# Rotary embedding on one core: hand-placed semaphores, eight of sixteen positions a batch summed on TensorE, and one signed GpSimd product per tile

## The chip, the cores and the metric

The kernel runs on one core of a Trainium2 chip. The time is in device microseconds of one execution, here the median of several runs. A core has TensorE (PE in the profile, its weight loads are PEld), VectorE (DVE), ScalarE (ACT), GpSimd (POOL) and SyncE (SP). SP and ACT also issue the DMAs here; their queues appear as SPq and ACTq, and 16 DMA engines move the data.

## The reference

```python
def reference(x, cos, sin):        # x: 8 x 2048 x 8 x 64, cos and sin: 2048 x 32, all f32
    x1 = x[..., : x.shape[-1] // 2]
    x2 = x[..., x.shape[-1] // 2 :]
    cos = cos[None, :, None, :]
    sin = sin[None, :, None, :]
    out1 = x1 * cos - x2 * sin
    out2 = x1 * sin + x2 * cos
    return np.concatenate([out1, out2], axis=-1)
```

Each of the 8 batches has 2048 positions of 8 heads of 64 numbers. The first 32 numbers of a head are x1, the last 32 x2. So the output is x times cosine, plus x with its halves exchanged times sine, with the sign of the first half turned. The input is 33.55 MB and so is the output.

## The kernel before

Position index q x 16 + r lies on partition q, so that each of the 128 partitions holds 16 positions of a batch, 512 numbers (2 KB) each: 32 KB in a row, in SBUF and in memory. A batch is one tile `xt` of 128x8192, of which there are five (`NBUF`), and it is rotated in place. The loads of batches 0 to 4 are issued by SP at the start (line 67; batch 0 in three parts); the load of batch b + 5 is issued after batch b's work and waits until batch b's store has left the buffer. Stores (line 74) are issued by ACT, those of the last batch by SP. The first batch is stored in shares of 2, 6 and 8 positions (4, 12 and 16 KB a partition), the last in shares of 8, 4 and 4, the others whole.

A batch is worked in pieces, of four positions mostly (`UNIT`, 2048 columns). Each piece is of one of three kinds, and `kinds` names the five that aren't A:

- A: GpSimd makes the sine products in two instructions, one per half of the heads (line 124), into an SBUF tile `t2`; VectorE makes the cosine product into the PSUM tile `t1` (line 131) and adds both into `xt` (line 138).
- B (batches 2, 4, 5, first piece): the cosine product goes to SBUF instead, and TensorE adds: two matmuls with the identity `eye` accumulate t1 and t2 in a PSUM tile `o` of 1024 columns (lines 145, 146), and ScalarE copies it back into `xt` (line 147).
- C (batches 1, 3, first piece): VectorE makes the sine product too (line 150), without exchange or sign; TensorE reads the crossed halves, with `eye` or the negative `neye` (lines 162, 163), and ScalarE copies (line 167).

There is one buffer of `o`, so a sum waits for the copy before it. A matmul of 512 columns of f32 shows as two records in the profile. The order of instructions on each engine is the order of the program (`keep`); the semaphores between engines are placed by the framework. Small tables are made at the start: `nsin`, `neye`, and copies of cosine and sine in PSUM (lines 92 to 95).

Of the kernel before, what the change touches and what calls it, by code (L numbers as in the profile page):

```python
# [9 lines left out]
@with_exitstack  # L10
def kernel(
    ctx: ExitStack,
    tc: tile.TileContext,
    x: bass.AP,
    cos: bass.AP,
    sin: bass.AP,
    out: bass.AP,
):
    nc = tc.nc
    keep = tc.keep_in_program_order  # L20
    f32 = mybir.dt.float32
    PSUM = bass.MemoryType.PSUM

    B, S, H, D = x.shape
    Dh = D // 2
    P = 128
    HD = H * D
    R = S // P
    ROW = R * HD
    UNIT = 4 * HD  # L30
    NBUF = 5
    C = 512
    last = B - 1

    xv = x.rearrange("b (q r) h d -> b q (r h d)", q=P)
    ov = out.rearrange("b (q r) h d -> b q (r h d)", q=P)
    cos_src = cos.rearrange("(q r) d -> q r d", q=P)
    sin_src = sin.rearrange("(q r) d -> q r d", q=P)

    const_pool = ctx.enter_context(tc.tile_pool(name="const", bufs=1))  # L40
    tab_pool = ctx.enter_context(tc.tile_pool(name="tab", bufs=1, space=PSUM))
    t1_pool = ctx.enter_context(tc.tile_pool(name="t1p", bufs=1, space=PSUM))
    o_pool = ctx.enter_context(tc.tile_pool(name="op", bufs=1, space=PSUM))
    t1s_pool = ctx.enter_context(tc.tile_pool(name="t1s", bufs=2))
    xpool = ctx.enter_context(tc.tile_pool(name="xpool", bufs=NBUF))
    t2_pool = ctx.enter_context(tc.tile_pool(name="t2p", bufs=3))

    cos_sb = const_pool.tile([P, R, Dh], f32, tag="cb")
    sin_sb = const_pool.tile([P, R, Dh], f32, tag="sb")
    nsin = const_pool.tile([P, R, Dh], f32, tag="ns")  # L50
    eye = const_pool.tile([P, P], f32, tag="eye")
    neye = const_pool.tile([P, P], f32, tag="neye")
    cos_ps = tab_pool.tile([P, R, Dh], f32, tag="cp")
    sin_ps = tab_pool.tile([P, R, Dh], f32, tag="sp")

    xts = {}

    def spans(sizes):
        lo = 0
        for n in sizes:  # L60
            yield lo, n
            lo += n

    def load(b):
        xt = xpool.tile([P, ROW], f32, tag="xt", name=f"xt{b}")
        for lo, n in spans([UNIT, UNIT, 2 * UNIT] if b == 0 else [ROW]):
            keep(nc.sync.dma_start(out=xt[:, lo : lo + n], in_=xv[b, :, lo : lo + n]))  # L67
            if b == 0 and lo == 0:
                keep(nc.sync.dma_start(out=cos_sb, in_=cos_src))
        xts[b] = xt  # L70

    def store(b, lo, n):
        queue = nc.sync if b == last else nc.scalar
        keep(queue.dma_start(out=ov[b, :, lo : lo + n], in_=xts[b][:, lo : lo + n]))  # L74

    keep(nc.scalar.dma_start(out=sin_sb, in_=sin_src))
    for b in range(NBUF):
        load(b)

    keep(nc.vector.addr_align(128))  # L80
    keep(nc.gpsimd.addr_align(128, offset=120))
    keep(nc.gpsimd.memset(eye, 0.0))  # L82
    nc.gpsimd.affine_select(
        out=eye,
        in_=eye,
        compare_op=mybir.AluOpType.not_equal,
        fill=1.0,
        base=0,
        pattern=[[-1, P]],
        channel_multiplier=1,  # L90
    )
    keep(nc.scalar.mul(nsin, sin_sb, -1.0))  # L92
    keep(nc.scalar.copy(sin_ps, sin_sb))  # L93
    keep(nc.scalar.mul(neye, eye, -1.0))
    keep(nc.vector.tensor_copy(cos_ps, cos_sb))  # L95

    def rep(a, n):
        return dataclasses.replace(a, ap=[a.ap[0][:], a.ap[1][:], [0, n], a.ap[-1][:]])

    kinds = {}  # L100
    for b, kind in ((1, "C"), (2, "B"), (3, "C"), (4, "B"), (5, "B")):
        kinds[(b, 0)] = kind

    def rotate(b, lo, n):
        kind = kinds.get((b, lo), "A")
        xt = xts[b][:, lo : lo + n]
        r0 = lo // HD
        nr = n // HD
        xk = xt.rearrange("p (r k d) -> p r k d", r=nr, d=Dh)
        xu = xt.rearrange("p (g u d) -> p g u d", u=2, d=Dh)  # L110
        if kind == "A":
            t1 = t1_pool.tile([P, n], f32, tag="t1")
        else:
            t1 = t1s_pool.tile([P, n], f32, tag="t1s")
        if kind == "C":
            t2 = t1s_pool.tile([P, n], f32, tag="t1s")
        else:
            t2 = t2_pool.tile([P, n], f32, tag="t2")
        t1u = t1.rearrange("p (g u d) -> p g u d", u=2, d=Dh)
        t2u = t2.rearrange("p (g u d) -> p g u d", u=2, d=Dh)  # L120
        if kind != "C":
            for u, tab in ((1, sin_sb), (0, nsin)):
                keep(
                    nc.gpsimd.tensor_mul(  # L124
                        out=t2u[:, :, u, :].rearrange("p (r h) d -> p r h d", h=H),
                        in0=xu[:, :, 1 - u, :].rearrange("p (r h) d -> p r h d", h=H),
                        in1=rep(tab[:, r0 : r0 + nr, :], H),
                    )
                )
        keep(  # L130
            nc.vector.tensor_mul(  # L131
                out=t1.rearrange("p (r k d) -> p r k d", r=nr, d=Dh),
                in0=xk,
                in1=rep(cos_ps[:, r0 : r0 + nr, :], 2 * H),
            )
        )
        if kind == "A":
            keep(nc.vector.tensor_add(out=xt, in0=t1, in1=t2))  # L138
        elif kind == "B":
            for j in range(n // (2 * C)):  # L140
                o = o_pool.tile([P, 2 * C], f32, tag="o")
                for k in range(2):
                    cs = slice((2 * j + k) * C, (2 * j + k + 1) * C)
                    oc = o[:, k * C : (k + 1) * C]
                    nc.tensor.matmul(oc, eye, t1[:, cs], start=True, stop=False)  # L145
                    nc.tensor.matmul(oc, eye, t2[:, cs], start=False, stop=True)  # L146
                keep(nc.scalar.copy(xt[:, 2 * j * C : 2 * (j + 1) * C], o))  # L147
        else:
            keep(
                nc.vector.tensor_mul(  # L150
                    out=t2.rearrange("p (r k d) -> p r k d", r=nr, d=Dh),
                    in0=xk,
                    in1=rep(sin_ps[:, r0 : r0 + nr, :], 2 * H),
                )
            )
            G = C // Dh
            for u in range(2):
                o = o_pool.tile([P, n // 2], f32, tag="o")
                for j in range(n // 2 // C):
                    oc = o[:, j * C : (j + 1) * C]  # L160
                    gs = slice(j * G, (j + 1) * G)
                    nc.tensor.matmul(oc, eye, t1u[:, gs, u, :], start=True, stop=False)  # L162
                    nc.tensor.matmul(  # L163
                        oc, eye if u else neye, t2u[:, gs, 1 - u, :], start=False, stop=True
                    )
                keep(
                    nc.scalar.copy(  # L167
                        xu[:, :, u, :], o.rearrange("p (g d) -> p g d", d=Dh)
                    )
                )  # L170

    def pieces(b):
        if b == 0:
            return [2 * HD, 2 * HD, UNIT, UNIT, UNIT]
        if b == last:
            return [UNIT, UNIT, UNIT, 2 * HD, 2 * HD]
        return [UNIT] * 4

    def shares(b):
        if b == 0:  # L180
            return [2 * HD, UNIT + 2 * HD, 2 * UNIT]
        if b == last:
            return [2 * UNIT, UNIT, UNIT]
        return [ROW]

    for b in range(B):
        done = 0
        outs = list(spans(shares(b)))
        for lo, n in spans(pieces(b)):
            rotate(b, lo, n)  # L190
            done = lo + n
            while outs and sum(outs[0]) <= done:
                store(b, *outs.pop(0))
        if b + NBUF <= last:
            load(b + NBUF)


# [28 lines left out]
```

## Time and profile before

| | |
|---|---|
| median of 3 runs | 163.44 us (163.33 to 163.69) |
| profiled execution, its own time | 163.48 us |
| its span | 161.7 us |
| VectorE busy | 140.1 us (87%) |
| GpSimd busy | 138.8 us (86%) |
| TensorE busy | 49.6 us (31%) |
| ScalarE busy | 12.8 us (8%) |
| bytes moved by the DMA engines | 67.65 MB, 418 GB/s over the span |

All times in the views are microseconds from the start of the span. The page has the busy share of each engine in 40 equal slices (a digit is tenths; the granted TensorE clock and the DMA's share are given in the same way), the chain of waits that ended last, and groups of instructions: line, engine, operation, output from inputs, shapes, count, busy time, mean duration in ns, then the idle time before them and what ended it. The timeline lists start, duration and instruction. A DMA issue shows on its queue with its line.

### The profile page before, as it was taken

The page shows a single profiled execution, that of the slowest core. Times are in us where ns is not written, and L with a number is a line of the kernel's source. Part 1 is how long each engine was busy: PE and PEld are TensorE (multiplying, and loading weights), DVE is VectorE, ACT ScalarE, POOL GpSimd, SP SyncE. Part 2 cuts the span into 40 slices and gives each one's busy share as a digit, 9 for nine tenths or more (in the row PEclk, how much of TensorE's full clock was granted, in tenths as well). Part 3 has the DMA queues.
Part 4 walks back from the last instruction along what each step waited for, and adds up shares of the span by engine and source line. Part 5 has one row for each costly group of instructions (what it writes and reads, how often), then busy time and mean ns, then how long its engine had stood idle before and what let it go on. Part 6 is the DMA issues. An engine that isn't in the chain of part 4 may idle for free.

```text
span 161.7 us, 573 instructions
## 1 busy us (share of the span) xinstructions
PE 49.6 (31%) x80; PEld 18.7 (12%) x80; DVE 140.1 (87%) x66; ACT 12.8 (8%) x14; POOL 138.8 (86%) x70
## 2 busy tenths in 40 slices
PE   0000000597309760978049723973000000000000
PEld 0000000142004220322023302320000000000000
DVE  0297999999999999999999999199989999899950
ACT  3300000002200220021100220022000000000000
POOL 1399994999999999992999979999799997999800
PEclk9999999999975998589956995599655555555555
DMA  5999999999999999999999999999999999999995
GB/s 184 418 432 438 420 428 405 444 409 489 397 401 450 438 462 397 438 462 397 438 462 397 438 462 397 438 470 389 438 470 389 438 470 397 430 470 397 405 420 213
DMA packets 3458, 67.65 MB, mean 418 GB/s; under 512 B 384, under 2 KB 384, under 8 KB 768
## 3 DMA queue, kind: packets, MB, share of 16 engines
q1 hardware_dynamic: 2016, 38.01, 55.4%
q10 hardware_dynamic: 1440, 29.62, 42.7%
q14 instruction: 2, 0.02, 0.0%
HBM read 34.08 MB, written 33.55 MB: 418 GB/s over the span
## 4 chain that ended last, share of the span: by engine, by line
DMA 48%; DVE 37%; POOL 9%; issue 2%; DVEq 0%; SPq 0%; POOLq 0%; ACTq 0%
DMA xt<-in_x_dram 26%; DMA out_dram<-xt 19%; DVE t L131 18%; DVE xt L138 17%; POOL t L124 9%; DMA sin_sb<-in_sin_dram 4%; DVE t L150 1%; DVEq L138 0%; SPq L67 0%; POOLq L124 0%; ACTq L74 0%
## 5 line engine op out<-in xcount | busy, mean ns | idle before, releaser
L124 POOL TENSOR_TENSOR t<-xt,sin_sb 128x1024 f32<-128x1024 f32 (+1 forms) x32 | 70.5, 2203 | 11.3 <-DMA xt<-in_x_dram 5.2
L131 DVE TENSOR_TENSOR t<-xt,cos_ps 128x2048 f32<-128x2048 f32 (+1 forms) x34 | 73.4, 2167 | 0.8
L124 POOL TENSOR_TENSOR t<-xt,nsin 128x1024 f32<-128x1024 f32 (+1 forms) x32 | 70.5, 2202 | 0.0
L138 DVE TENSOR_TENSOR xt<-t,t 128x2048 f32<-128x2048 f32 (+1 forms) x29 | 62.2, 2145 | 8.0 <-POOL t L124 5.4
L145 PE MATMUL o<-t,eye 128*128 128x512 f32 x24 | 17.2, 807 | 22.9 <-DVE t L131 19.5
L162 PE MATMUL o<-t,eye 128*128 128x512 f32 x16 | 12.1, 847 | 37.7 <-DVE t L131 35.5
L146 PE MATMUL o<-t,eye 128*128 128x512 f32 x24 | 14.9, 709 | 0.0
L147 ACT COPY xt<-o 128x1024 f32<-128x1024 f32 x6 | 6.1, 1012 | 45.7 <-PE o L146 45.7
L145 PEld LDWEIGHTS o<-t,eye 128*128 128x128 f32 x24 | 5.6, 257 | 32.3 <-issue 26.4
L162 PEld LDWEIGHTS o<-t,eye 128*128 128x128 f32 x16 | 3.7, 256 | 43.1 <-issue 39.3
L167 ACT COPY xt<-o 128x1024 f32<-128x1024 f32 x4 | 4.0, 1012 | 47.8 <-PE o L163 36.8
L95 DVE COPY cos_ps<-cos_sb 128x512 f32<-128x512 f32 x1 | 0.7, 695 | 6.9 <-DMA cos_sb<-in_cos_dram 6.9
L146 PEld LDWEIGHTS o<-t,eye 128*128 128x128 f32 x24 | 5.7, 239 | 8.2 <-issue 7.7
L163 PE MATMUL o<-t,neye 128*128 128x512 f32 x8 | 6.3, 882 | 0.2 <-DVE t L150 0.2
L150 DVE TENSOR_TENSOR t<-xt,sin_ps 128x2048 f32<-128x2048 f32 x2 | 4.6, 2281 | 0.0
L163 PE MATMUL o<-t,eye 128*128 128x512 f32 x8 | 4.1, 592 | 0.0
L163 PEld LDWEIGHTS o<-t,neye 128*128 128x128 f32 x8 | 2.2, 306 | 5.3 <-issue 3.7
L82 POOL MEMSET eye<- 128x128 f32 x1 | 0.2, 204 | 2.4 <-issue 2.4
L163 PEld LDWEIGHTS o<-t,eye 128*128 128x128 f32 x8 | 1.5, 190 | 1.9 <-issue 1.9
L92 ACT ACT_TABLE_LOAD x1 | 1.3, 1283 | 1.2 <-PEq L210 1.2
L92 ACT ACTIVATE nsin<-sin_sb 128x512 f32<-128x512 f32 x1 | 0.6, 629 | 4.0 <-DMA sin_sb<-in_sin_dram 4.0
L93 ACT COPY sin_ps<-sin_sb 128x512 f32<-128x512 f32 x1 | 0.6, 579 | 0.0
(6 smaller groups left out, 1.0 us busy)
## 6 DMA issues: line engine op xcount, KB each, us to landing
xt<-in_x_dram SPq DMA_DIRECT2D x7, 4096.0 KB, 41.4
out_dram<-xt ACTq DMA_DIRECT2D x6, 4096.0 KB, 28.6
xt<-in_x_dram SPq DMA_DIRECT2D x2, 1024.0 KB, 6.9
xt<-in_x_dram SPq DMA_DIRECT2D x1, 2048.0 KB, 13.1
out_dram<-xt ACTq DMA_DIRECT2D x1, 2048.0 KB, 25.8
out_dram<-xt SPq DMA_DIRECT2D x1, 2048.0 KB, 10.0
out_dram<-xt SPq DMA_DIRECT2D x2, 1024.0 KB, 6.3
out_dram<-xt ACTq DMA_DIRECT2D x1, 1536.0 KB, 20.7
```

The lines of the kernel that those rows point to most:

```text
L92: keep(nc.scalar.mul(nsin, sin_sb, -1.0))
L95: keep(nc.vector.tensor_copy(cos_ps, cos_sb))
L124: nc.gpsimd.tensor_mul(out=t2u[:, :, u, :].rearrange("p (r h) d -> p r h d", h=H), in0=xu[:, :, 1 - u, :].rearrange("p (r h) d -> p r h d" ...
L131: nc.vector.tensor_mul(out=t1.rearrange("p (r k d) -> p r k d", r=nr, d=Dh), in0=xk, in1=rep(cos_ps[:, r0 : r0 + nr, :], 2 * H),)
L138: keep(nc.vector.tensor_add(out=xt, in0=t1, in1=t2))
L145: nc.tensor.matmul(oc, eye, t1[:, cs], start=True, stop=False)
L146: nc.tensor.matmul(oc, eye, t2[:, cs], start=False, stop=True)
L147: keep(nc.scalar.copy(xt[:, 2 * j * C : 2 * (j + 1) * C], o))
L150: nc.vector.tensor_mul(out=t2.rearrange("p (r k d) -> p r k d", r=nr, d=Dh), in0=xk, in1=rep(sin_ps[:, r0 : r0 + nr, :], 2 * H),)
L162: nc.tensor.matmul(oc, eye, t1u[:, gs, u, :], start=True, stop=False)
L163: nc.tensor.matmul(oc, eye if u else neye, t2u[:, gs, 1 - u, :], start=False, stop=True)
L167: nc.scalar.copy(xu[:, :, u, :], o.rearrange("p (g d) -> p g d", d=Dh))
```

## The change

The framework's placement of semaphores is replaced by semaphores placed by hand, inside one critical section: `Count` holds a semaphore and what it has been raised to, and `wait` makes an engine wait for such a point. Buffers are fixed: one `t2` of four quarters of 2048 columns, one `t1` and one `o` in PSUM; a plan for each batch gives kind, first position, number of positions, and quarter.

- Eight positions of batches 0 to 6 and four of batch 7 are summed on TensorE: in odd batches one C piece of eight positions, in even ones two B pieces of four. The cosine product of a B or C piece is written over `xt`; TensorE reads `xt` and `t2`.
- GpSimd makes the sine products of a piece in one instruction, from a table `sgn` that holds the negative and the positive sine side by side, and with a backward step over the halves of `xt`. The first piece of batch 0 is still made in two.
- Batch 0 is stored in four shares of four positions (8 KB a partition), in the order 0, 4, 12, 8.
- ScalarE copies the cosine table instead of VectorE; two alignment calls are dropped; SP waits for the last stores at the end.

Core of the diff (`Count` counts, `repeat`, `region` and `products` give views of a table, of `xt` and of `t2`):

```diff
-    t1_pool = ctx.enter_context(tc.tile_pool(name="t1p", bufs=1, space=PSUM))
-    o_pool = ctx.enter_context(tc.tile_pool(name="op", bufs=1, space=PSUM))
-    t1s_pool = ctx.enter_context(tc.tile_pool(name="t1s", bufs=2))
...
+    t2 = sb("t2", [4 * UNIT])
+    t1 = psum.tile([P, UNIT], f32, tag="t1", name="t1")
+    cos_ps = psum.tile([P, R, Dh], f32, tag="cp", name="cos_ps")
+    sin_ps = psum.tile([P, R, Dh], f32, tag="sp", name="sin_ps")
+    o = psum.tile([P, 2 * C], f32, tag="o", name="o")
...
+    def wait(engine, point):
+        engine.wait_ge(point[0].sem, point[1])
+    crit = tc.tile_critical(no_gpsimd_drain=True)
+    crit.__enter__()
+    dve, prod, mm, act = (Count(n) for n in ("dve", "prod", "mm", "act"))
+    pair = [Count(f"pair{i}") for i in range(4)]
+    landed = {}
+    stored = {}
+    read = [None] * 4
+    known = {"gpsimd": set(), "vector": set()}
...
     def load(b):
+        parts = [(0, 4), (4, 4), (8, 8)] if b == 0 else [(0, R)]
+        if b >= NBUF:
+            for point in stored[b - NBUF]:
+                wait(nc.sync, point)
+        for lo, n in parts:
+            cols = slice(lo * HD, (lo + n) * HD)
+            ins = nc.sync.dma_start(out=xts[b % NBUF][:, cols], in_=xv[b, :, cols])
+            point = Count(f"ld{b}_{lo}").by(ins, 16)
+            for r in range(lo, lo + n):
+                landed[(b, r)] = point
             if b == 0 and lo == 0:
-                keep(nc.sync.dma_start(out=cos_sb, in_=cos_src))
-        xts[b] = xt
-    def store(b, lo, n):
-        queue = nc.sync if b == last else nc.scalar
-        keep(queue.dma_start(out=ov[b, :, lo : lo + n], in_=xts[b][:, lo : lo + n]))
-    keep(nc.scalar.dma_start(out=sin_sb, in_=sin_src))
-    for b in range(NBUF):
+                cos_in = Count("cos_in").by(nc.sync.dma_start(out=cos_sb, in_=cos_src), 16)
+        return cos_in if b == 0 else None
+    def store(b, lo, n, needs):
+        engine = nc.sync if b == last else nc.scalar
+        for point in needs:
+            wait(engine, point)
+        cols = slice(lo * HD, (lo + n) * HD)
+        ins = engine.dma_start(out=ov[b, :, cols], in_=xts[b % NBUF][:, cols])
+        stored.setdefault(b, []).append(Count(f"st{b}_{lo}").by(ins, 16))
...
-    keep(nc.vector.addr_align(128))
-    keep(nc.gpsimd.addr_align(128, offset=120))
...
-    keep(nc.scalar.mul(nsin, sin_sb, -1.0))
-    keep(nc.scalar.copy(sin_ps, sin_sb))
-    keep(nc.scalar.mul(neye, eye, -1.0))
-    keep(nc.vector.tensor_copy(cos_ps, cos_sb))
+    wait(nc.scalar, sin_in)
+    nsin_done = act.by(nc.scalar.mul(sgn[:, :, 0, :], sin_sb, -1.0))
+    wait(nc.scalar, cos_in)
+    cos_done = act.by(nc.scalar.copy(cos_ps, cos_sb))
+    sgn_done = act.by(nc.scalar.copy(sgn[:, :, 1, :], sin_sb))
+    sin_done = act.by(nc.scalar.copy(sin_ps, sin_sb))
+    wait(nc.scalar, eye_done)
...
+    def sines(b, lo, n, buf, count):
+        xt = region(b, lo, n)
+        if read[buf]:
+            wait(nc.gpsimd, read[buf])
+        if landed[(b, lo)] not in known["gpsimd"]:
+            known["gpsimd"].add(landed[(b, lo)])
+            wait(nc.gpsimd, landed[(b, lo)])
+        if (b, lo) == (0, 0):
+            xu = xt.rearrange("p (g u d) -> p g u d", u=2, d=Dh)
+            tu = products(buf, n).rearrange("p (g u d) -> p g u d", u=2, d=Dh)
+            for u, tab in ((1, sin_sb), (0, sgn[:, :, 0, :])):
+                wait(nc.gpsimd, sin_in if u else nsin_done)
+                done = count.by(
                     nc.gpsimd.tensor_mul(
+                        out=tu[:, :, u, :].rearrange("p (r h) d -> p r h d", h=H),
                         in0=xu[:, :, 1 - u, :].rearrange("p (r h) d -> p r h d", h=H),
+                        in1=repeat(tab[:, lo : lo + n, :], H),
                     )
                 )
+            wait(nc.gpsimd, sgn_done)
+            return done
+        x5 = xt.rearrange("p (r h u d) -> p r h u d", r=n, h=H, u=2)
+        swapped = dataclasses.replace(
+            x5, offset=x5.offset + Dh, ap=[d[:] for d in x5.ap[:3]] + [[-Dh, 2], x5.ap[4][:]]
+        )
+        return count.by(
+            nc.gpsimd.tensor_mul(
+                out=products(buf, n).rearrange("p (r h u d) -> p r h u d", r=n, h=H, u=2),
+                in0=swapped,
+                in1=repeat(sgn[:, lo : lo + n], H),
             )
         )
...
+    def times(out, table, b, lo, n):
+        return nc.vector.tensor_mul(
+            out=out.rearrange("p (r k d) -> p r k d", r=n, d=Dh),
+            in0=region(b, lo, n).rearrange("p (r k d) -> p r k d", r=n, d=Dh),
+            in1=repeat(table[:, lo : lo + n, :], 2 * H),
+        )
+    t1_read = cos_done
+    self_known = 0
+    copied = neye_done
+    def vector_waits(*points):
+        nonlocal self_known
+        for point in points:
+            if point in known["vector"] or (point[0] is dve and point[1] <= self_known):
+                continue
+            if point[0] is dve:
+                self_known = point[1]
+            wait(nc.vector, point)
+    def on_vector(b, lo, n, buf):
+        nonlocal t1_read
+        sines(b, lo, n, buf, pair[buf])
+        vector_waits(landed[(b, lo)], t1_read)
+        known["vector"].add(landed[(b, lo)])
+        wait(nc.vector, pair[buf].by(times(t1[:, : n * HD], cos_ps, b, lo, n)))
+        t1_read = read[buf] = dve.by(
+            nc.vector.tensor_add(out=region(b, lo, n), in0=t1[:, : n * HD], in1=products(buf, n))
+        )
+        return t1_read
+    def on_tensor(b, lo, n, buf, crossed=False):
+        nonlocal copied
+        if crossed:
+            vector_waits(landed[(b, lo)], *read[buf : buf + n // 4], sin_done)
+            made = dve.by(times(products(buf, n), sin_ps, b, lo, n))
+            vector_waits(made)
         else:
+            made = sines(b, lo, n, buf, prod)
+            wait(nc.vector, made)
+        known["vector"].add(landed[(b, lo)])
+        wait(nc.tensor, dve.by(times(region(b, lo, n), cos_ps, b, lo, n)))
+        for j in range(0, n, 2):
+            wait(nc.tensor, copied)
+            cs = slice(j * HD, (j + 2) * HD)
+            xj, tj = region(b, lo, n)[:, cs], products(buf, n)[:, cs]
+            pattern = "p (u g d) -> p u g d" if crossed else "p (g u d) -> p g u d"
+            if crossed:
+                xu = xj.rearrange("p (g u d) -> p u g d", u=2, d=Dh)
+                tu = tj.rearrange("p (g u d) -> p u g d", u=2, d=Dh)
+            for k in range(2):
+                oc = o[:, k * C : (k + 1) * C]
+                xk = xu[:, k] if crossed else xj[:, k * C : (k + 1) * C]
+                tk = tu[:, 1 - k] if crossed else tj[:, k * C : (k + 1) * C]
+                nc.tensor.matmul(oc, eye, xk, start=True, stop=False)
+                sign = neye if crossed and k == 0 else eye
+                ins = nc.tensor.matmul(oc, sign, tk, start=False, stop=True)
+            summed = mm.by(ins)
+            wait(nc.scalar, summed)
+            out = xu if crossed else xj
+            src = o.rearrange("p (u g d) -> p u g d", u=2, d=Dh) if crossed else o
+            copied = act.by(nc.scalar.copy(out, src))
+            read[buf + j // 4] = summed
+        return copied
+    wait(nc.tensor, eye_done)
+    for b in range(B):
         if b == 0:
+            plan = [("A", 0, 4, 0), ("B", 4, 4, 2), ("B", 8, 4, 3), ("A", 12, 4, 1)]
+            shares = [(0, 4), (4, 4), (12, 4), (8, 4)]
+        elif b == last:
+            plan = [("B", 0, 4, 2), ("A", 4, 4, 0), ("A", 8, 4, 1), ("A", 12, 4, 0)]
+            shares = [(0, 8), (8, 4), (12, 4)]
+        elif b % 2:
+            plan = [("C", 0, 8, 0), ("A", 8, 4, 2), ("A", 12, 4, 3)]
+            shares = [(0, R)]
+        else:
+            plan = [("B", 0, 4, 2), ("A", 4, 4, 0), ("B", 8, 4, 3), ("A", 12, 4, 1)]
+            shares = [(0, R)]
+        done = {}
+        for kind, lo, n, buf in plan:
+            point = on_vector(b, lo, n, buf) if kind == "A" else on_tensor(b, lo, n, buf, kind == "C")
+            for r in range(lo, lo + n):
+                done[r] = point
+            while shares and all(r in done for r in range(shares[0][0], sum(shares[0]))):
+                s0, sn = shares.pop(0)
+                needs = {}
+                for r in range(s0, s0 + sn):
+                    count, v = done[r]
+                    needs[count] = max(v, needs.get(count, 0))
+                store(b, s0, sn, needs.items())
         if b + NBUF <= last:
             load(b + NBUF)
+    for b in range(last + 1 - NBUF, B):
+        for point in stored[b]:
+            wait(nc.sync, point)
+    crit.__exit__(None, None, None)
```

## The prediction

> **What bounds the kernel now.** I read the slices and the chain of waits first, then TensorE's and ScalarE's timeline, then the stretches at the end.
>
> ```profile
> DMA  5999999999999999999999999999999999999995
> ...
> DMA packets 3458, 67.65 MB, mean 418 GB/s; under 512 B 384, under 2 KB 384, under 8 KB 768
> ...
> DMA 48%; DVE 37%; POOL 9%; issue 2%; DVEq 0%; SPq 0%; POOLq 0%; ACTq 0%
> ```
>
> The 16 DMA engines are full in all 40 slices but the first and the last. 67.65 MB at 418 GB/s is the span, 161.7 us. The chain that ended last runs through loads, stores and vector work in turn, so compute (DVE 140.1 us busy, POOL 138.8) only just keeps up. No edit can make the bytes fewer; an edit gains little and loses whatever stops the DMA.
>
> ```profile
> 155.00:156.00 1.00, 0.00 (x0) 0.00 (x0) 0.83 (x1) 0.00 (x0) 0.00 (x0) 0.50 0.99 418
> ...
> 159.00:160.00 1.00, 0.00 (x0) 0.00 (x0) 0.00 (x0) 0.00 (x0) 0.00 (x0) 0.50 0.65 270
> 160.00:161.00 1.00, 0.00 (x0) 0.00 (x0) 0.00 (x0) 0.00 (x0) 0.00 (x0) 0.50 0.02 8
> ```
>
> In this view by stretches the last two columns are the DMA share and GB/s. The data end at 159.65 (0.65 of that microsecond), so a tail of 161.70 - 159.65 = 2.05 us follows the last byte. From 140 to 156, stores nearly alone, the rate is 422 to 425 GB/s; I use 425. In the first 4 us the core moved 174 GB/s x 4 = 0.70 MB, worth 1.6 us at full rate, so 2.4 us were lost; the first issue was at 0.74, so a queue that starts empty costs 2.4 - 0.74, about 1.6 us.
>
> What the change loads most is TensorE with ScalarE. Their timeline in one of the five pieces summed there today:
>
> ```profile
> 48.52 2.05 PE L145 MATMUL o<-t,eye 128*128 128x512 f32 x2 [6.73 <-DVE t L131]
> 50.36 1.91 PE L146 MATMUL o<-t,eye 128*128 128x512 f32 x2
> 52.07 1.58 PE L145 MATMUL o<-t,eye 128*128 128x512 f32 x2
> 53.48 1.02 PE L146 MATMUL o<-t,eye 128*128 128x512 f32 x2
> 55.65 1.12 PE L145 MATMUL o<-t,eye 128*128 128x512 f32 x2 [1.15 <-ACT xt L147]
> 56.62 1.02 PE L146 MATMUL o<-t,eye 128*128 128x512 f32 x2
> 57.47 1.02 PE L145 MATMUL o<-t,eye 128*128 128x512 f32 x2
> 58.33 1.02 PE L146 MATMUL o<-t,eye 128*128 128x512 f32 x2
> ```
>
> ```profile
> 54.59 1.01 ACT L147 COPY xt<-o 128x1024 f32<-128x1024 f32 x1 [11.74 <-PE o L146]
> 59.39 1.01 ACT L147 COPY xt<-o 128x1024 f32<-128x1024 f32 x1 [3.79 <-PE o L146]
> ```
>
> Columns: start, duration, what, and the idle time before it. A tile is 1024 columns (two positions). There is one o buffer, so TensorE waits out the copy (1.15 us idle) and ScalarE waits out the sum (3.79): the two take turns. A warm tile has a period of 59.39 - 54.59 = **4.80 us**. The crossed pieces have the same period (copies at 37.03 and 41.83, 71.41 and 76.22). The first tile of a piece is slow: 6.07 us from first matmul to copy, not 3.74.
>
> **The change, part by part.**
>
> *More positions on TensorE.* Today five pieces of four positions, ten tiles. After: batch 0 sums 8 positions, batches 1 to 6 sum 8 each, batch 7 sums 4: 60 positions, **30 tiles**, still one o, still an explicit wait of TensorE for the copy. 30 x 4.80 = 144 us in one serial chain, 19.2 us a batch. That is nearly the time that the DMA needs for a batch (8.39 MB at 425 GB/s, 19.7 us); the chain cannot win time back, and it starts late and has a tail.
>
> *Where it starts.* POOL's first (split) product runs 6.49 to 8.77 to 11.05 (two 128x1024 forms, 2.28 us apart on the timeline). The first TensorE piece, positions 4 to 7, needs the signed product, then the vector product, which now writes x in place and so must wait for POOL.
>
> ```profile
> L131 DVE TENSOR_TENSOR t<-xt,cos_ps 128x2048 f32<-128x2048 f32 x30 | 68.5, 2292 | 0.7
> L124 POOL TENSOR_TENSOR t<-xt,sin_sb 128x1024 f32<-128x1024 f32 x28 | 65.5, 2339 | 8.2 <-DMA xt<-in_x_dram 5.2 <-DVE xt L138 3.0
> L124 POOL TENSOR_TENSOR t<-xt,sin_sb 128x512 f32<-128x512 f32 x4 | 5.0, 1256 | 3.1 <-DMA sin_sb<-in_sin_dram 3.1
> ```
>
> The signed product, 128x2048 in one instruction, is not in the trace. The two POOL rows give 2339 - 1256 = 1083 ns per 512 elements; three more steps on 1256 give 4.50 us, two halves give 4.56. Bounds: as fast as VectorE, 2.29, or twice its price for the backward step, 9.1. I take 4.56, since inner runs (32 elements) and elements are those of today. So 11.05 + 4.56 = 15.6, + 2.35 (2.29 and a semaphore) = 18.0. First copy at 18.0 + 6.07 = 24.0, done at 25.0.
>
> *Is it kept fed?* Each piece's data against the moment when TensorE is free for it: batch 0 second piece 22.5 against 29.8; batch 1: its load lands near 27.3 as now, two vector products of 4.48 (4096 elements at the slope of the rows) give 36.3 against 39.4; batch 2 51.9 and 61.0 against 58.6 and 68.2. From there it repeats: the last plain piece of batch 2 waits for t2 buffer 1, which TensorE frees at 57.5, is added at 65.7, and then VectorE makes batch 3's 8 positions by 74.7 against 77.8; batch 5 111.9 against 116.2; batch 7 150.9 against 154.6. The leads are 3 to 9 us: narrow, never negative. So the chain has no gap: last copy ends at 25.0 + 29 x 4.80 = **164.2**.
>
> *The last stores.* Batch 6's store needs the 28th copy, 154.6. Batch 7's first store, positions 0 to 7, contains its summed piece and heads SP's queue, so the other two stores stand behind it though their adds end near 160 and 165: all 4.19 MB go after 164.3. The DMA idles before 154.7 (batch 5's store, issued at 135.4, is done by 135.5 + 1.6 + 9.9 = 147). Then 154.7 + 1.6 + 8.39 MB / 425 GB/s (19.7) = 176.0, + 2.05 = span **178.1**. The span now is 161.70 inside an execution of 163.48, so 1.78 lies around it: **179.9 us**, against that execution's 163.48 and the median's 163.44.
>
> The Trainium skill, "DMA: Bandwidth & Descriptors", section "Where 436 GB/s comes from", says that HBM to SBUF transfers bind near 358 GB/s. By it the last 8.39 MB would take 23.4 us and the sum would be 183.6. This trace, with 418 GB/s over the whole span, disagrees.
>
> *What costs nothing, and why.* VectorE falls from 61 large products and sums to 55 (some 126 us for 140), POOL from 32 to 26 (117 for 139): both now wait on TensorE's buffers, so nothing is gained. Positions 0 to 3 are stored together, at about 13.5 and not 10.25, and batch 0's last piece goes at 39.4 instead of 27.8, since ScalarE, which issues stores, has the four copies ahead of it. Load 5 waits for these: about 61 instead of 53.66. The cover is loads 1 to 4, in the queue until 21.5 + 4.2 MB are moved (61); load 5 lands near 80, and its first product starts after 100. Without that cover the DMA would idle some 2 us. Cos copied by ScalarE: ready at 7.65, VectorE now starts at 7.64. The dropped alignment calls have no row; the "issue" gaps in the chain are 0.02 to 0.07 us, I take 0.
>
> *Hand-placed waits.* Semaphore hops in a tile are 0.04 and 0.05 us now. If they vanished, 30 x 0.09 = 2.7 us are won; if each becomes 0.06 longer, 3.6 are lost. I take 0 and keep both ends.
>
> **Rivals.**
>
> *The clock falls back in the chain.* If every piece starts with a slow tile, as all five now do, 14 x (6.07 - 3.70) = 33 us are added: copies end at 197.4, then 1.7 + 9.9 + 2.05 + 1.78: 212.8. For: the granted clock is 0.50 from 48.5 to 53 and 0.99 from 53 to 60.4. Against: the slow tiles follow pauses of over 5 us; after the 1.1 us pauses every second tile was fast, and the new chain has only those.
> The Trainium skill, "TensorE: Matmul & The Clock Gate", section "A second HAM failure mode: psum-queue depth-cycling", says that short pauses between groups on PSUM buffers can make the clock swing; by it this rival, or part of it, comes. Ten tiles of this trace do not show it.
>
> *The signed product is dearer.* At 6.0 us POOL gates the pieces: last copies at 159.5 (batch 6) and 169.1, giving 184.8. At 9.1, POOL sets the pace, the last add ends at 240.9, and 248.9 follows.
>
> *The chain does not bind (no slower).* Place: the o buffer between TensorE and ScalarE. If the period were at most 4.24 us, copies would end by 148.1 and the 4.19 MB behind them (1.7 + 9.9 + 2.05) at 161.7; then the full DMA decides again: about 163.4, or some tenths less for the faster last batch. It needs the copy to run beside the next sum. For: 3.70 and 1.01 apart would fit. Against: the wait is written out, and the pause is in the trace. The matmul count would show whether 30 tiles were indeed summed.
>
> **Numbers.** Gap-free chain 0.76, 179.9 (own range 176 to 185: waits, rate between 418 and 442, a microsecond at the start). Product near 6 us 0.07 (184.8), at 9.1 0.03 (248.9); clock 0.09 (212.8); chain hidden 0.05 (163.4). The range 175 to 188 holds the first two, nearly all of 0.83. A difference under 0.2% can't be told from none in this kernel; faster by more has 0.03 and within it 0.02, both from the last case, slower 0.95.
>
> **What would show it.** Right: 30 copies on ScalarE, 4.80 us apart, idle before them put down to TensorE; DMA share falling below 0.9 from about 130; SP's last three stores issued together at 164. Wrong at the start: the first copy far from 24. Wrong in the middle: gaps in the copies (VectorE or POOL late), or a POOL product off 4.5 us. Wrong altogether: DMA full to the end with copies under 4.3 us apart.

## The result and the profile after

The changed kernel takes 181.40 us (median of 4 runs, 180.73 to 181.92); the kernel before, run beside it, takes 163.51. The ratio is 1.109, with a 95% interval of 1.105 to 1.114. The profiled execution took 181.72, its span is 179.3.

The first view is the page of the changed kernel, busy tenths in 40 slices of 4.5 us, then the totals of the DMA.

```profile
PE   0000977777777888777777777778887777774000
...
PEclk9999999999999999999999999999999999999755
DMA  5999999999999989999999999999908850499991
...
DMA packets 3602, 67.67 MB, mean 377 GB/s; under 512 B 400, under 2 KB 400, under 8 KB 656
```

The bytes are the same (67.67 MB), but the DMA row has holes: from slice 30 on the engines are idle, then full, then idle. TensorE is busy at an even 0.7 to 0.8 from slice 6 to slice 36, and the granted clock reads full all that time.

Four groups of the same page, the costliest first:

```profile
L169 POOL TENSOR_TENSOR t<-xt,sgn 128x2048 f32<-128x2048 f32 x25 | 112.8, 4532 | 38.0 <-PE o L235 38.0
L233 PE MATMUL o<-xt,eye 128*128 128x512 f32 x120 | 65.0, 624 | 51.2 <-ACT xt L240 30.6
L240 ACT COPY xt<-o 128x1024 f32<-128x1024 f32 x30 | 30.4, 1012 | 124.8 <-PE o L235 124.8
L177 DVE TENSOR_TENSOR xt<-xt,cos_ps 128x2048 f32<-128x2048 f32 (+1 forms) x12 | 33.9, 2821 | 24.5 <-POOL t L169 24.4
```

There are the 30 copies. ScalarE idled 124.8 us ahead of them, all of it waiting for TensorE's sums, and TensorE idled 30.6 us waiting for the copies: each waits for the other. The signed product takes 4.53 us, and GpSimd now idles 38.0 us for quarters of `t2` that TensorE has still to read: the engine that was 86% busy waits for the one that was 31% busy.

ScalarE's timeline, its first four copies and the last four:

```profile
23.41 1.01 ACT L240 COPY xt<-o 128x1024 f32<-128x1024 f32 x1 [14.22 <-PE o L235]
28.22 1.01 ACT L240 COPY xt<-o 128x1024 f32<-128x1024 f32 x1 [3.79 <-PE o L235]
...
33.08 1.01 ACT L240 COPY xt<-o 128x1024 f32<-128x1024 f32 x1 [3.85 <-PE o L235]
37.88 1.01 ACT L240 COPY xt<-o 128x1024 f32<-128x1024 f32 x1 [3.79 <-PE o L235]
...
148.91 1.01 ACT L240 COPY xt<-o 128x1024 f32<-128x1024 f32 x1 [3.85 <-PE o L235]
153.71 1.01 ACT L240 COPY xt<-o 128x1024 f32<-128x1024 f32 x1 [3.79 <-PE o L235]
154.75 0.34 ACTq L103 DMA_DIRECT2D out_dram<-xt  x1
158.58 1.01 ACT L240 COPY xt<-o 128x1024 f32<-128x1024 f32 x1 [3.85 <-PE o L235]
163.38 1.01 ACT L240 COPY xt<-o 128x1024 f32<-128x1024 f32 x1 [3.79 <-PE o L235]
```

The idle time ahead of a copy is 3.79 us, or 3.85 at the start of a piece, from the second copy to the last: a period of 4.80 or 4.86 us, without one gap in 140 us. Batch 6's store leaves at 154.75, right behind the 28th copy.

The last stretches (the columns are those of the view shown of before: engines' busy times, granted clock, DMA share, GB/s):

```profile
130.00:135.00 5.00, 3.70 (x8) 1.44 (x8) 2.81 (x2) 1.21 (x2) 4.41 (x2) 1.00 0.08 33
135.00:145.00 10.00, 7.37 (x16) 2.88 (x16) 5.65 (x3) 2.36 (x3) 4.87 (x2) 1.00 0.98 419
145.00:155.00 10.00, 7.50 (x17) 3.04 (x18) 6.33 (x3) 2.08 (x3) 10.00 (x3) 1.00 0.00 0
155.00:165.00 10.00, 7.24 (x16) 2.71 (x16) 9.63 (x5) 2.02 (x2) 7.08 (x2) 1.00 0.97 415
```

Batch 5's store fills the DMA from 135 to 145, then there is nothing to store until 155. About 15 us of an idle DMA, from 130 on, are most of what the change costs.

### The profile page after: what moved, and what is told of

It is laid out like the page before. It is cut to its first block, busy times and chain, and to the rows that moved or that the text cites. A ratio compares the mean times of both kernels' runs of the same rounds, so it can differ in the third digit from the quotient of the medians.

```text
span 179.3 us, 716 instructions
## 1 busy us (share of the span) xinstructions
PE 112.1 (63%) x240; PEld 43.8 (24%) x240; DVE 124.1 (69%) x49; ACT 34.1 (19%) x36; POOL 118.1 (66%) x33
## 2 busy tenths in 40 slices
DMA packets 3602, 67.67 MB, mean 377 GB/s; under 512 B 400, under 2 KB 400, under 8 KB 656
## 4 chain that ended last, share of the span: by engine, by line
PE 30%; DVE 28%; POOL 22%; ACT 6%; DMA 3%; issue 3%; DVEq 0%; SPq 0%; POOLq 0%
POOL t L169 20%; PE o L233 16%; PE o L235 14%; DVE t L177 11%; DVE xt L204 9%; DVE xt L177 7%; ACT xt L240 6%; DMA xt<-in_x_dram 3%; POOL t L156 2%; DVEq L71 0%; POOLq L71 0%; SPq L301 0%; SPq L74 0%
## 5 line engine op out<-in xcount | busy, mean ns | idle before, releaser
L169 POOL TENSOR_TENSOR t<-xt,sgn 128x2048 f32<-128x2048 f32 x25 | 112.8, 4532 | 38.0 <-PE o L235 38.0
L233 PE MATMUL o<-xt,eye 128*128 128x512 f32 x120 | 65.0, 624 | 51.2 <-ACT xt L240 30.6
L240 ACT COPY xt<-o 128x1024 f32<-128x1024 f32 x30 | 30.4, 1012 | 124.8 <-PE o L235 124.8
L177 DVE TENSOR_TENSOR xt<-xt,cos_ps 128x2048 f32<-128x2048 f32 (+1 forms) x12 | 33.9, 2821 | 24.5 <-POOL t L169 24.4
L177 DVE TENSOR_TENSOR t<-xt,cos_ps 128x2048 f32<-128x2048 f32 x17 | 39.0, 2291 | 8.2 <-ACT cos_ps L126 8.0
L204 DVE TENSOR_TENSOR xt<-t,t 128x2048 f32<-128x2048 f32 x17 | 39.0, 2292 | 7.7 <-POOL t L169 6.4
L233 PEld LDWEIGHTS o<-xt,eye 128*128 128x128 f32 x120 | 20.7, 192 | 89.5 <-issue 50.8
L177 DVE TENSOR_TENSOR t<-xt,sin_ps 128x4096 f32<-128x4096 f32 x3 | 13.3, 4422 | 0.3
L235 PE MATMUL o<-t,neye 128*128 128x512 f32 x24 | 12.3, 592 | 0.0
L235 PEld LDWEIGHTS o<-t,neye 128*128 128x128 f32 x24 | 4.6, 190 | 5.7 <-issue 5.7
```

What stands on the lines that cost most here:

```text
L169: nc.gpsimd.tensor_mul(out=products(buf, n).rearrange("p (r h u d) -> p r h u d", r=n, h=H, u=2), in0=swapped, in1=repeat(sgn[:, lo : lo + ...
L177: return nc.vector.tensor_mul(out=out.rearrange("p (r k d) -> p r k d", r=n, d=Dh), in0=region(b, lo, n).rearrange("p (r k d) -> p r k d", ...
L204: nc.vector.tensor_add(out=region(b, lo, n), in0=t1[:, : n * HD], in1=products(buf, n))
L233: nc.tensor.matmul(oc, eye, xk, start=True, stop=False)
L235: ins = nc.tensor.matmul(oc, sign, tk, start=False, stop=True)
L240: copied = act.by(nc.scalar.copy(out, src))
```

## Experiments

Times are medians; ratios are against the kernel before on the same chip, with 95% intervals.

| kernel | us | ratio |
|---|---|---|
| changed kernel | 181.40 | 1.109 (1.105 to 1.114) |
| five pieces on TensorE, rest as changed | 165.04 | 1.0099 (1.0062 to 1.0136) |
| sum buffer in two halves | 166.13 | 1.0171 (1.0140 to 1.0202) |
| two halves, small first stores | 165.28 | 1.0122 (1.0106 to 1.0137) |
| batch 7 on VectorE | 179.62 | 1.1015 (1.0962 to 1.1068) |
| one more GpSimd product a piece | 182.73 | 1.1183 (1.1154 to 1.1212) |
| half copies (half of each sum isn't copied) | 168.47 | 1.0326 (1.0292 to 1.0360) |
| before + 8 KB first stores | 164.19 | 1.0044 (1.0029 to 1.0060) |
| before + signed product | 163.47 | 1.0003 (0.9992 to 1.0013) |
| before + eight positions | 180.22 | 1.1017 (1.0982 to 1.1052) |
| before + eight positions, two halves | 169.28 | 1.0368 (1.0343 to 1.0393) |

**Take the positions away, keep the rest.**

```diff
+        q = [("A", 0, 4, 0), ("A", 4, 4, 1), ("A", 8, 4, 2), ("A", 12, 4, 3)]
+        if b in (1, 3):
+            q[0] = ("C", 0, 4, 0)
+        elif b in (2, 4, 5):
+            q[0] = ("B", 0, 4, 0)
```

> Everything of the change is kept but the number of positions on TensorE: again five pieces of four (first piece of batches 1 to 5), ten tiles in place of 30. Theory T (the turn-taking of TensorE and ScalarE on one sum buffer, 30 tiles of 4.80 us, sets the end): the chain leaves the path, the DMA is full to the end, 163.5 to 165.0 us. Rival S (hand-placed waits, critical section, signed product or 8 KB stores cost the time): 175 to 181 us.

Measured 165.04 (just above theory T's range, far from rival S; batch 0's shares go in the order 0, 4, 8, 12 here). The slices of its page show the DMA full again:

```profile
DMA  4999999999899799899999899999999999999991
```

**Add the positions alone.** The kernel before, framework semaphores and split products kept (part of the edit; a crossed piece's sine product also moves ahead of its cosine product, which is now in place):

```diff
+    for b in range(B):
+        if b % 2 and b != last:
+            kinds[(b, 0)] = kinds[(b, UNIT)] = "C"
+        else:
+            kinds[(b, UNIT if b == 0 else 0)] = "B"
+            if b != last:
+                kinds[(b, 2 * UNIT)] = "B"
...
-            t1 = t1s_pool.tile([P, n], f32, tag="t1s")
+            t1 = xt
```

> The kernel before with one part of the change: eight positions a batch (four in the last) summed on TensorE, cosine product written in place; the framework's semaphores, split products and first stores stay, one sum buffer. Theory T: 30 tiles of 4.80 us in turns, 178 to 186 us (gaps may come from the fewer product buffers). Rival S (the hand-placed semaphores cost most): 164 to 168 us.

Measured 180.22. Its last copies on ScalarE:

```profile
154.91 1.01 ACT L160 COPY xt<-o 128x1024 f32<-128x1024 f32 x1 [3.79 <-PE o L159]
155.95 0.34 ACTq L74 DMA_DIRECT2D out_dram<-xt  x1
159.71 1.01 ACT L160 COPY xt<-o 128x1024 f32<-128x1024 f32 x1 [3.79 <-PE o L159]
164.51 1.01 ACT L160 COPY xt<-o 128x1024 f32<-128x1024 f32 x1 [3.79 <-PE o L159]
```

With other semaphores, other buffers and other products the chain has the same period and ends within 1.2 us of the same moment. So the 30 tiles are worth nearly the whole loss (16.8 of 17.9 us), with or without the hand-placed waits. One caution: in this kernel GpSimd and VectorE end late too. The last add ends at 173.51, the last store leaves at 173.87, and the page's chain has 55% on GpSimd. The DMA is full from 157 to 177 behind batch 6's store, so the two paths end at about the same time. The last experiment shows how long the second one takes without the turn-taking.

**Take the turn-taking away.** In the changed kernel each half of `o` gets its own wait and copy:

```diff
             for k in range(2):
+                wait(nc.tensor, copied[k])
                 oc = o[:, k * C : (k + 1) * C]
...
+                summed = mm.by(nc.tensor.matmul(oc, sign, tk, start=False, stop=True))
+                wait(nc.scalar, summed)
+                src = oc.rearrange("p (g d) -> p g d", d=Dh) if crossed else oc
+                copied[k] = act.by(nc.scalar.copy(xk, src))
```

> The changed kernel with its sum buffer used as two halves of 512 columns: TensorE sums into one half while ScalarE copies the other (two copies of some 0.58 us for one of 1.01). Same positions, same products. Theory T: a tile takes TensorE's 3.4 to 3.7 us alone, 30 tiles some 105 us, the chain leaves the path: 163.5 to 167 us. Rival R (GpSimd and VectorE, tied through the four product buffers, set the pace, as half of the chain that ended last lies on them): not under 175 us.

Measured 166.13, as theory T had it. The timeline of its copies:

```profile
26.12 0.59 ACT L236 COPY xt<-o 128x512 f32<-128x512 f32 x1 [1.13 <-PE o L233]
27.84 0.59 ACT L236 COPY xt<-o 128x512 f32<-128x512 f32 x1 [1.13 <-PE o L233]
...
29.55 0.59 ACT L236 COPY xt<-o 128x512 f32<-128x512 f32 x1 [1.13 <-PE o L233]
```

A half has a period of 1.72 us, a tile 3.43: TensorE's eight records of 0.43 and nothing else. The 1.0 us of copy and the other 0.4 us of a 4.80 us tile are both off the chain, and 15 us of the 18 come back. The same numbers of products, sums, positions and stores are done, so what cost the time is the wait for the one buffer. The DMA is full again:

```profile
DMA  5999899989989989989999999999999999999994
```

**Shorten the wait.** (Half of each copy is left out.)

```diff
-            copied = act.by(nc.scalar.copy(out, src))
+                copied = act.by(nc.scalar.copy(out[:, 0], src[:, 0]))
...
+                copied = act.by(nc.scalar.copy(out[:, :C], src[:, :C]))
```

> The changed kernel with ScalarE copying only half of each sum (512 of 1024 columns; the other half of the summed positions keeps its cosine product). The period of a tile falls by 0.43 to some 4.37 us. Theory T: 29 x 0.43 = 12.5 us off the chain, last copy of batch 6 near 143, and 143 + 1.7 + 19.7 + 2.5 + 2.4 gives 169.5: 168 to 171 us. Rival D (ScalarE's copies lie beside other work): 180 to 182 us.

Measured 168.47. Its copies are 4.38 to 4.44 us apart and batch 6's store leaves at 143.31 (143 was expected). 0.43 us off each tile took 11.4 us off the store and 12.9 us off the time; the other 1.5 us fit the end, where the changed kernel's trace has one DMA engine finishing late (see batch 7 below) and this one has not.

**Load the engine that the chain of waits names.** The chain that ended last, by engine, is on the changed kernel's page:

```profile
PE 30%; DVE 28%; POOL 22%; ACT 6%; DMA 3%; issue 3%; DVEq 0%; SPq 0%; POOLq 0%
```

By these shares GpSimd and VectorE carry half of the path. The run puts one more product ahead of each of 18.

```diff
+                nc.gpsimd.tensor_mul(
+                    out=spare.rearrange("p (r h u d) -> p r h u d", r=1, h=H, u=2),
...
+                    in1=repeat(sgn[:, lo : lo + 1], H),
```

> The changed kernel with one more GpSimd product of 128x512 (some 1.2 us, into a tile that nobody reads) ahead of each of the 18 products of batches 1 to 6, 21 us of work more. Theory T: TensorE's data stay 2 us or more ahead, copies stay 4.80 us apart, 181.4 us within 0.7. Rival R (GpSimd is on the path, as the chain that ended last has 22% on it): six of these products lie on that chain, 7 us more, 188 us or above.

Measured 182.73, 1.3 us above the changed kernel: neither the 0 of theory T nor the 7 of rival R. The groups of GpSimd and two copies of ScalarE, in this kernel:

```profile
L184 POOL TENSOR_TENSOR t<-xt,sgn 128x2048 f32<-128x2048 f32 x25 | 113.1, 4531 | 0.4 <-PE o L250 0.4
L175 POOL TENSOR_TENSOR spare<-xt,sgn 128x512 f32<-128x512 f32 x18 | 23.0, 1277 | 17.5 <-PE o L250 17.3
```

```profile
24.94 1.01 ACT L255 COPY xt<-o 128x1024 f32<-128x1024 f32 x1 [15.60 <-PE o L250]
...
78.02 1.01 ACT L255 COPY xt<-o 128x1024 f32<-128x1024 f32 x1 [3.79 <-PE o L250]
...
83.15 1.01 ACT L255 COPY xt<-o 128x1024 f32<-128x1024 f32 x1 [4.12 <-PE o L250]
```

23.0 us of work were added and GpSimd's idle time fell by 20 us (38.0 to 17.9). On ScalarE the idle time ahead of the crossed piece of batch 3 grows from 3.85 to 4.12 us, and the same happens once more, by 0.2, in batch 5. That is 0.5 us in all. In the changed kernel VectorE ends batch 3's crossed products at 73.03 and TensorE comes to them at 77.65, a lead of 4.6 us; from 39.46, where a wait of GpSimd ends, five of the added products stand on the way there, 6.1 us. Of these, 1.2 fill waits that the changed kernel has there, and the other 4.9 eat the lead up. In the profiled executions batch 6's store leaves 2.0 us later (156.75 for 154.75): 0.5 by these gaps and 1.5 at the start, where the first copy comes at 24.94 and not at 23.41. The added products, the first of them at 29.79, can't have caused that (see the last section); whether the other executions started late as well isn't known.

**Clear the last batch from TensorE.** Batch 7's first piece becomes kind A.

```diff
-            plan = [("B", 0, 4, 2), ("A", 4, 4, 0), ("A", 8, 4, 1), ("A", 12, 4, 0)]
+            plan = [("A", 0, 4, 2), ("A", 4, 4, 0), ("A", 8, 4, 1), ("A", 12, 4, 3)]
```

> The changed kernel with batch 7 wholly on VectorE: 28 tiles. Theory T: the end comes from batch 6's store, which still goes at 154.7 with 8.39 MB to move from there: 154.7 + 1.6 + 19.7 + 2.3 + 2.4 = 180.7, so 180 to 182 us, no gain from two tiles fewer. Rival H (the summed piece of batch 7, at the head of SP's queue, holds back its 4.19 MB): some 9 us less, 171 to 174 us.

Measured 179.62, just under theory T's range and 6 us above rival H's. Batch 6's store leaves at 154.90 (154.75 in the changed kernel), so two tiles fewer hardly matter. Some 1.8 us do come back, and the ends of the two traces show where. In the changed kernel nearly all data are through by 175.7, but the last packets follow one after another, 8 KB in 0.31 us, until 177.6, as if one of the 16 engines were late. From 176 to 177 the share is 0.08, at 33 GB/s:

```profile
176.00:177.00 1.00, 0.00 (x0) 0.00 (x0) 0.00 (x0) 0.00 (x0) 0.00 (x0) 0.50 0.08 33
```

Here the last packet ends at 175.5. SP's three stores now leave one after the other over 9.6 us instead of together at 164.4; whether that is why no engine is late was not tried.

**The small parts alone**, in the kernel before. First the stores, then the product (part of its edit; the table `sgn` is made, and the cosine table moves into a product tile):

```diff
-            return [2 * HD, UNIT + 2 * HD, 2 * UNIT]
+            return [UNIT] * 4
```

> The kernel before with one part of the change: batch 0 worked in four pieces of four positions and stored in four shares of 8 KB a partition, in order. Theory T: hidden under the loads of batches 1 to 4; within 0.4 us of 163.4. Rival F (the later first store and later load 5 leave the DMA short, and explain why the changed kernel stays 2 to 3 us behind even when its chain is off the path): 165 us or more.

```diff
-            for u, tab in ((1, sin_sb), (0, nsin)):
+            x5 = xt.rearrange("p (r h u d) -> p r h u d", r=nr, h=H, u=2)
+            swapped = dataclasses.replace(
+                x5, offset=x5.offset + Dh, ap=[d[:] for d in x5.ap[:3]] + [[-Dh, 2], x5.ap[4][:]]
+            )
```

> The kernel before with one part of the change: one signed GpSimd product a piece (the first piece still in two). A product takes 4.53 us against two of 2.28 apart, so nothing is won or lost on GpSimd. Theory T: within 0.4 us of 163.4. Rival G (longer products hold VectorE's sums back where the halves did not): 164.5 us or more.

The product is worth nothing (ratio 1.0003, 0.9992 to 1.0013). The stores cost 0.44%, 0.7 us, less than rival F had and more than theory T allowed: load 5 goes at 63.73 instead of 53.66. The DMA stays full around that time, so the loss isn't a plain gap. What carries it to the end stays open.

**What is left with the chain off the path.** First the changed kernel with the two halves; the edit on top of them:

```diff
-            plan = [("A", 0, 4, 0), ("B", 4, 4, 2), ("B", 8, 4, 3), ("A", 12, 4, 1)]
-            shares = [(0, 4), (4, 4), (12, 4), (8, 4)]
+            plan = [("A", 0, 2, 0), ("A", 2, 2, 1), ("B", 4, 4, 2), ("B", 8, 4, 3), ("A", 12, 4, 0)]
+            shares = [(0, 2), (2, 6), (8, 8)]
```

> The hand-placed kernel with two halves of the sum buffer, and batch 0 stored in shares of 2, 6 and 8 positions as before. If the first stores' 0.7 to 0.8 us add to the rest: 165.2 to 165.6 us (166.1 less 0.7 or so). If the hand-placed kernel's rest of 2.7 us is of another kind: 165.9 to 166.4 us, no gain.

Measured 165.28: the first stores' share adds up, though the two ratios' intervals all but touch. 1.9 us remain against the kernel before. Some 0.4 of them lie outside the span (time less span is 2.16 to 2.27 here, 1.74 to 1.85 in the kernel before). The span itself is 162.9 for 161.7: 0.2 go with the later first issue (0.94 for 0.74), and some 0.5 with the time from the end of the last data packet to the end of the span (1.7 for 1.2). The other 0.5 isn't explained.

Then the two halves in the framework's kernel, on top of the eight positions (part of the edit):

```diff
-    o_pool = ctx.enter_context(tc.tile_pool(name="op", bufs=1, space=PSUM))
+    o_pool = ctx.enter_context(tc.tile_pool(name="op", bufs=2, space=PSUM))
```

> The framework's kernel with eight positions a batch on TensorE (as in the run before of that kind), and the sum buffer as two halves of 512 columns. Theory T: the chain leaves the path and the full DMA sets the end again, 163.0 to 164.5 us. Rival Q (eight positions on TensorE cost by themselves, through buffers held longer or by SBUF traffic): 165.5 us or more, as in the hand-placed kernel with two halves (166.1).

Measured 169.28, a miss: the two halves take 11 us off 180.22 but do not bring the framework's kernel back to 163.4. (One `o` of 512 columns per sum, two buffers.) Its DMA has holes again near the end:

```profile
DMA  5999999999899999998999999998989994599966
```

A line of its list of waits (us in all, times, the longest):

```profile
POOL t L129 <- DVE xt L151: 29.7, 9, 9.0
```

That kernel has three product tiles where the changed kernel has four quarters. GpSimd waits 29.7 us, up to 9.0 at a time, for VectorE to add a product and free its tile, and the last add ends at 162.35 (155.84 in the kernel before, 148.69 in the hand-placed one with two halves). So rival Q's "buffers held longer" fits there. That the fourth quarter and the spread order of kinds spare the hand-placed kernel this is an argument from the waits: no run gave the framework's kernel a fourth product tile. No kernel of this study beats the one before.

## Why the prediction was right, and where it was off

It gave 179.9, range 175 to 188; 181.40 was measured. Point by point:

- **The chain.** 30 tiles, period 4.80, no gap: shown by the copies, and by the runs that put the same 30 tiles into the other kernel (180.22) and that took only the turn-taking away (166.13). First copy 23.41 (24.0 was worked out), last one done at 164.39 (164.2). The hops of 0.06 at the start of a piece add up to 0.7 us (11 of them), and an earlier start paid for them. That was luck: the first matmul came at 18.23 (18.0), and the first tile took 5.2 us and not 6.07, a time that differs between traces (see the last section).
- **The end.** Batch 6's store left at 154.75 (154.7), SP's stores from 164.42 (164.3), and the DMA was empty before 155. But the terms "1.6 + 19.7" and "2.05" were of the wrong sizes, in both directions. The first packets start at 155.6, 0.85 us after the issue and not 1.6. Nearly all of the 8.39 MB are then through by 175.7, some 20 us, but the late engine goes on until 177.6. The 2.05 was counted from 159.65 in the kernel before, where the last data packet ends at 160.5, so that 1.2 us followed; here it is 1.7. From the issue to the end of the span the sum had 23.35 us, and 24.55 were measured.
- **What lies around.** 2.42 us outside the span for 1.78. Together with the point above: 1.2 + 0.6 = 1.8, which is 181.72 less 179.9.
- **What was to cost nothing.** The signed product: right, 4.53 us and no difference. The first stores: wrong by 0.7 us; "The cover is loads 1 to 4" holds for gaps in the DMA, but the run shows a loss without one. The hand-placed waits: the "semaphore hops" in a tile stayed as they were, but time less span grew, and so did the time behind the last packet, which the prediction didn't price.
- **Kept fed.** No gap appeared. The lead of batch 3's crossed piece was 4.6 us (3.1 was worked out); 1.28 us more per product opened gaps of 0.2 to 0.3 us.
- **The rivals.** The clock did not fall back: from the second tile to the last a sum takes the same time, at a granted clock of 1.00. So what the Trainium skill says of short pauses ("TensorE: Matmul & The Clock Gate", section "A second HAM failure mode: psum-queue depth-cycling"), which the prediction named, did not show here with pauses of 1.1 us. That rival's price was also too high: the change makes 12 pieces, so 11 and not 14 could start slow behind the first, 26 us and not 33. The product was not dearer. "The chain does not bind" can now be priced: it takes two halves of the buffer, and then the DMA binds, as that rival said, at 165 to 166 and not at 163.4.

## What to carry to other kernels

Two engines that hand one buffer back and forth finish one tile in the sum of both their times (here 4.80 us), however idle each looks; before moving work to such a pair, multiply that period by the tiles it will get and compare the product with the span, start and final stores included. Splitting the buffer in two costs ScalarE some 0.2 us more a tile (two copies of 0.59 for one of 1.01) and took 15 of 18 us back here, 11 of 17 in the framework's kernel, where waits for product tiles were left. In the chain that ended last, a share held by an engine that waits for freed buffers is no price: 23 us more work on GpSimd, which held 22% of that chain, cost 1.3 us, and the trace shows gaps of only half a microsecond that come from it.

## What the runs showed of the hardware that was not expected

The first tile's speed varies between traces. Up to it the changed kernel, the one with batch 7 on VectorE, the one with half copies and the one with added products have the same instructions. TensorE started at 18.23, 18.09, 18.41 and 18.36, and the first copy came 5.2, 5.5, 5.5 and 6.6 us later, as more or fewer of the first matmuls took twice as long (two records in 2.04 us instead of 1.02). Some 3 to 6 us after the start all four ran at full speed and stayed there through 1.1 us pauses (0.7 with half copies) for the rest of the kernel. The granted clock reads 1.00 in all this time, in the slow first matmuls as well: it does not show them, and the lengths of the records do.

At the end of the changed kernel one engine's worth of packets came 2 us behind all others, and so it is, by 1.7 us, with the added products; the other traces of the kernels that end by the chain of copies have at most 0.6 us of it. What decides it stays open.

Time less span isn't a constant of the chip: 1.74 to 1.90 us with the framework's semaphores (2.16 once), 1.90 to 2.53 with the hand-placed ones (3.32 once). What in the hand-placed kernel lengthens it was not tried.
